# A hybrid diffusion step on one core: the modulation vectors summed over row blocks on ACT, POOL and DVE instead of in TensorE's accumulation

## The chip, the core and the metric

One core of one Trainium2 chip. Its engines are TensorE (PE, with its weight loads PEld), VectorE (DVE), ScalarE (ACT), GpSimd (POOL) and SyncE (SP, which here issues all transfers); SBUF and PSUM are the on-chip memories. The time of a run is the device time in microseconds; lower is better.

## The reference, cut to what matters

Two layers of a backbone run on 128 context tokens and 512 latent tokens of 1024 features. Each layer has three branches (a bidirectional S5, a windowed and a global attention), which gates merge, then an output projection, a norm, a squared-ReLU MLP of 4096 and a norm. Six modulation vectors of 1024 values each come from a conditioning vector, one for the context tokens and one for the latent tokens:

```
m = jax.nn.silu(cond) @ w_mod + b_mod          # cond: 1024 values; w_mod: 1024 x 6144; 2 conds
sh1, sc1, g1, sh2, sc2, g2 = split(m, 6)
h  = x * (1 + sc1) + sh1                       # before the input projection
x  = layer_norm(alpha * x + g1 * f)
h2 = x * (1 + sc2) + sh2                       # before the MLP
x  = layer_norm(alpha * x + g2 * (relu(h2 @ w_up) ** 2 @ w_down))
```

All is float32.

## The kernel before

The kernel is written layer by layer: `phase_a` holds everything up to the merged branches, `phase_b` the output projection, the MLP and the two norms. Weights come in packed tiles of 128x1024 (512 KB). `raw_tile` (line 112) loads one into a ring of four buffers, which all weights share in program order; `wtile` (line 126) splits it into a high part, written by ACT (line 123), and the exact rest, written by DVE (line 124), and every product with activations is three matmuls, high by high, high by low and low by high (lines 159 to 161 and 170 to 172). The modulation is not split: its matmuls (line 187) take float32 as it is.

`mods_steps` (line 175) makes the vectors. It is a generator: its caller takes one step at a time beside other work. A round is 2048 columns (two vectors); a step is one row block k of 128 rows, two raw tiles. `scond[:, k, :]` holds the conditioning vectors after SiLU, 128 rows by 32 columns, of which two are not zero. Four matmuls a step, each with 32 result partitions (a quarter q of the round's columns, at partitions 32q) and 512 columns, multiply it by the raw tile. In the second layer the eight steps accumulate in one PSUM bank and ACT copies the sums out (line 192). In the first layer (`acc=True`) each step has a bank of its own, and DVE adds it to the row so far (line 190). Then four transposes (line 197) and an add of the bias (line 198) put the vectors on the partitions, and the two gates also go to DRAM as rows (lines 203 to 211).

The first two vectors of the first layer are made elsewhere (`mods0`, line 516, untouched). `mods_steps` makes its other two rounds as the `side` of `branch` (line 1072), which takes a step after each of its 16 products: first for the window branch, which runs among the blocks of the global attention, then for the S5 branch. For the second layer it makes all three rounds during the first layer's MLP: `ahead` (line 1253) takes a step beside most weight tiles, in turn with the tables of the S5 branch (`s5_prep`, line 274) while these last. Those tables use DVE, POOL and PE.

[...] In the MLP `pg` hands out `g` and `sc` banks.

The order of each engine's instructions isn't the order of the code: `TileContext(..., schedule_with_timeline_sim=True)` has a planner lay out every engine's queue beforehand, by a simulated timeline in which earlier code goes first. On the chip each queue then runs in that fixed order.

Of the kernel before, what the change touches and what calls it, by code (L numbers as in the profile page):

```python
# [15 lines left out]
NT = 5                      # token tiles of 128: 0 the prompt, 1..4 the sample  # L16
D = 1024
NCH = 84                    # chunk columns: [pad, 16 prompt, pad, pad, 64 sample, pad]
# [5 lines left out]
AHEAD = ((0, 1, 4, 2, 4, 1), (1, 0, 1, 2, 4, 1))   # gates worked out ahead: beside the queries, the scan, beside its outputs, around the GLU, by layer  # L24
# [3 lines left out]
SPLITS = ((0, 3), (3, 5))   # token-tile ranges of a feature-major product  # L28


def net(tc, I, O, depth=DEPTH, dbg=None):
# [37 lines left out]
    # ---------------------------------------------------------------- constants  # L69
# [19 lines left out]
    V.memset(mh, -0.5)  # L89
    scond = base.tile([128, 8, 32], F32, name="scond")  # L90
# [17 lines left out]
    # persistent work  # L108
# [8 lines left out]
    def split(hi, lo, src, half=False):  # L117
        """src (or src / 2) as a high part and the exact rest"""
        if half:
            S.activation(hi, src, AF.Copy, scale=0.5)  # L120
            V.scalar_tensor_tensor(lo, src, 0.5, hi, op0=ALU.mult, op1=ALU.subtract)
        else:
            S.activation(hi, src, AF.Copy)  # L123
            V.tensor_tensor(lo, src, hi, op=ALU.subtract)  # L124

    def wtile(src, K, slot=None):
        """a packed weight tile [128, 1024] of K row blocks as its high and low parts: [(hi, lo)] by row block"""
# [17 lines left out]
    def tok(a, t0, t1):  # L145
        """the token tiles t0..t1 of a view [128, NT, 128], or of the views of the two parts of SPLITS"""
        if not isinstance(a, tuple):
            return a[:, t0:t1, :]
        i = 0 if t0 < SPLITS[0][1] else 1
        return a[i][:, t0 - SPLITS[i][0]:t1 - SPLITS[i][0], :]  # L150

    def mm_fm(out, ws, acts, t0, t1, ks=None, first=True, last=True):
        """feature-major: out [128 f, tokens] += w[k].T @ act[k]; ws[k] = (hi, lo) [128, 128];
        acts[k] = (hi, lo) views of the tokens"""
# [8 lines left out]
    def mm_tm(out, ws, acts, t, first=True, last=True):  # L163
        """token-major: out [128 tok, n] += act[k][:, t].T @ w[k]; ws[k] = (hi, lo) [128, n]"""
# [9 lines left out]
    # ---------------------------------------------------------------- adaLN modulation  # L174
    def mods_steps(l, rounds, tmp, tmp2=None, acc=False):
        """the modulation vectors of a layer, 2048 columns a round, one row block of the weight a step"""
        if rounds[0] == 0:
            SY.dma_start(bmodT, I["bmodT"][:, l])
        for r in rounds:
            p = None if acc else ppv()  # L180
            mrow = tmp()
            for k in range(8):
                if acc:
                    p = pg()
                ws = [raw_tile(I["w_mod"][l, r, k, h]) for h in range(2)]
                for q in range(4):
                    T.matmul(p[32 * q:32 * q + 32, :], scond[:, k, :], ws[q // 2][:, (q % 2) * 512:(q % 2) * 512 + 512],
                             start=(acc or k == 0), stop=(acc or k == 7))
                if acc and k > 0:
                    V.tensor_tensor(mrow, mrow, p, op=ALU.add)  # L190
                elif acc or k == 7:
                    S.activation(mrow, p, AF.Copy)  # L192
                if k < 7:
                    yield
            pc = pg() if acc else ppv()
# [6 lines left out]
            # the gates as rows  # L202
            for q in range(4):
                vec = 2 * r + q // 2
                if vec in (2, 5):
                    P = slice(32 * q, 32 * q + 2)
                    brow = (tmp2 or tmp)()
# [6 lines left out]
    def affine(l, w):  # L214
        """affA/affB[l][:, w]: h = xhat * A + B; w 0: before w_in, 1: before w_up"""
# [11 lines left out]
    # ---------------------------------------------------------------- h: transposed, modulated, split  # L227
    def new_h():
        """high and low parts, each in the two parts of SPLITS"""
        return tuple(tuple(wp.tile([128, 8, t1 - t0, 128], F32R, name=n + str(i), tag=n + str(i), bufs=1)  # L230
                           for i, (t0, t1) in enumerate(SPLITS)) for n in ("hh", "hl"))

# [23 lines left out]
    # ---------------------------------------------------------------- layer norm of a token tile  # L256
    def ln_stat(st):
        """mean, rstd, - mean rstd from the bn_stats of the chunks"""
# [8 lines left out]
    def ln_tile(z, st):  # L267
        """z [128, 1024] -> (z - mean) * rstd in place; st: bn_stats of its chunks"""
# [4 lines left out]
    # ---------------------------------------------------------------- S5 tables (weights only)  # L273
    def s5_prep(l, pp, after=None, use=None):
# [25 lines left out]
        def poly(o, r, cs):  # L300
            """cs: from the highest power, to the constant"""
# [8 lines left out]
        def expm1(o, x, plus1=False):  # L310
            """exp(x) - 1 (or exp(x)): x = k ln2 + r"""
# [8 lines left out]
            tt(q, q, r, ALU.add)                       # e^r - 1  # L320
# [3 lines left out]
            p2 = ti.bitcast(F32)                       # 2^k  # L324
# [12 lines left out]
        # sin and cos - 1 of th: th = q 2pi + r, a = r/4, two doublings  # L337
# [19 lines left out]
        # powers of lam_bar: Pw[:, ri, k, g], k = 0..8; n = lam_bar - 1  # L357
# [27 lines left out]
        # b_bar = (lam_bar - 1) / lam * b  # L385
# [13 lines left out]
        # ec[t]: fwd lam^(t+1), bwd lam^(8-t);  ei[j]: fwd lam^(7-j), bwd lam^j  # L399
# [12 lines left out]
        for b in range(8):  # L412
# [31 lines left out]
            # C lam^e and its negated imaginary part  # L444
# [10 lines left out]
            # lag kernel of these four groups; stationary columns: [full | fwd | bwd]  # L455
# [15 lines left out]
            # input operator, built with states on partitions and transposed  # L471
# [20 lines left out]
    # ---------------------------------------------------------------- phase A  # L492
    def phase_a(l, h):
# [9 lines left out]
        if l == 0:  # L503
# [3 lines left out]
            # the rows of a partial sum over four row blocks: one from each strip  # L507
# [4 lines left out]
            # the first three row blocks of the S5 input go along  # L512
# [3 lines left out]
            def mods0(g_):  # L516
                """shift and scale of 256 features"""
# [57 lines left out]
        # entry states by chunk column, the backward direction turned round inside each segment  # L575
# [12 lines left out]
        def s5_in(b, io):  # L588
            """what the chunks of four groups add to the states"""
# [15 lines left out]
        # ---- S5 input, to the chunked layout  # L605
# [27 lines left out]
        def s5_states():  # L633
            """the states at the chunks' starts"""
# [6 lines left out]
            # ---- scan over chunks: entry[i + 1] = lam^8 entry[i] + v, prompt and sample side by side, in pairs:  # L641
            # w = lam^8 v[i] + v[i + 1]; entry[i + 2] = lam^16 entry[i] + w one after the other; the entries between them
# [11 lines left out]
            def pairs(src, dst):  # L654
                """dst + 2 k += lam^8 (src + 2 k), all 41 pairs of columns"""
# [26 lines left out]
            # final states of the prompt  # L682
            fin = sp.tile([128, 2, 2, 32], F32, name="fin", tag="sa", bufs=1)[:, 0].rearrange("p a b -> p (a b)")
            S.activation(fin, st[:, 17].rearrange("p a b -> p (a b)"), AF.Copy)
            # the backward direction back into chunk order
# [11 lines left out]
        # ---- k, v, q of the window branch  # L697
# [3 lines left out]
        # the rotation with the weights of the query norm, and the sums of squares of the queries  # L701
# [8 lines left out]
        def rope_apply(out, src, n, t, e, tab=None):  # L710
            """out[., h, 64] = src * C + swap(src) * S; src [128, n, 64], sample tile t - 1"""
# [14 lines left out]
        def chunk(name, i):  # L726
            """two packed tiles: the 256 columns i of a token-major weight, K = 1024"""
            return wtile(I[name][l, 2 * i], 4) + wtile(I[name][l, 2 * i + 1], 4)

        def kv_gemm(i, side=iter(())):  # L730
# [15 lines left out]
            if i == 1:  # L746
                # the norm of the keys
# [6 lines left out]
            # the rotation of the sample's keys  # L754
# [9 lines left out]
        def q_gemm(i, dst, side=iter(()), cs=(0, 1)):  # L764
            for c in cs:
                ws = chunk("w_q", 2 * i + c)
                for t in range(NT):
# [10 lines left out]
                    else:  # L778
                        # the norm's factor of a row and head goes with the scores
# [14 lines left out]
        def gate(i, ft, out_fn, side=iter(())):  # L794
            """tanh(gate / 2): sigmoid(gate) = (1 + that) / 2; the halves go with the sums"""
# [8 lines left out]
        def gates_ahead(i, fts):  # L804
            """gates ahead of their use, kept in DRAM; half a gate a step"""
# [25 lines left out]
        # ---- window attention, beside the scan  # L831
        # ---- attention
# [4 lines left out]
        def keys(i):  # L837
            """K^T high and low, on both partition halves; V as [high | low]"""
# [3 lines left out]
            # cached keys and values  # L842
# [20 lines left out]
        def queries(qt):  # L863
            """qt [128, 512] token-major -> scaled, transposed, by head: high and low part on the two partition halves"""
# [11 lines left out]
        def attend(i, t, qs, KH, KL, VV, y):  # L876
            """token tile t of branch i; y slab [128, NT, 4, 128]"""
# [6 lines left out]
            # contiguous runs of key columns  # L884
            runs = []
            n1 = 4 if len(blks) < 5 else 3          # blocks in a bank of their own; the two heads share one for the rest
# [7 lines left out]
            stat = atp[0].tile([128, 4, 8], F32, name="stat", tag="stat", bufs=2)      # -max | sums | second sums | 1 / sum  # L894
            ng, sm, sx, rs = (stat[:, j] for j in range(4))
            for v in range(2):
                po = ppv()
                for pr in range(2):
# [3 lines left out]
                    # a bank for each of the two heads, and one for what does not fit  # L902
# [53 lines left out]
                # the products with the high and the low part of v sit on the two partition halves  # L956
# [14 lines left out]
            # 1 / sum of each row, spread over the features of its head  # L971
# [25 lines left out]
        # gates of the window branch fill the tensor engine beside the scan  # L997
# [10 lines left out]
        # ---- outputs of the chunks  # L1008
# [35 lines left out]
        # ---- second half: the merged branches  # L1044
# [12 lines left out]
        def y_views(ft):  # L1057
            """(natural tokens [c, t], same of yT) for the prompt and the sample"""
# [415 lines left out]
```

## Time and profile before

| | |
|---|---|
| median of 3 timed runs | 2419.13 us (2417.3 to 2419.89) |
| span of the profiled execution | 2422.9 us |
| mean granted TensorE clock | 0.977 |
| busy: PE, DVE, ACT, POOL | 95%, 62%, 41%, 23% |
| moved by DMA | 278.25 MB, 115 GB/s |

The profiled execution has no time of its own beside its span, from its first to its last instruction. In the rows, L187 is line 187 of the kernel. `out<-in` gives tiles by name, `128x512` partitions by elements. [...] A row's idle time is that of the engine just before these instructions, with what ended it. Stretches are counted from the span's start.

### The profile page before, as it was taken

The page shows a single profiled execution, that of the slowest core. Times are in us where ns is not written, and L with a number is a line of the kernel's source. Part 1 is how long each engine was busy: PE and PEld are TensorE (multiplying, and loading weights), DVE is VectorE, ACT ScalarE, POOL GpSimd, SP SyncE. Part 2 cuts the span into 40 slices and gives each one's busy share as a digit, 9 for nine tenths or more (in the row PEclk, how much of TensorE's full clock was granted, in tenths as well). Part 3 has the DMA queues.
Part 4 walks back from the last instruction along what each step waited for, and adds up shares of the span by engine and source line. Part 5 has one row for each costly group of instructions (what it writes and reads, how often), then busy time and mean ns, then how long its engine had stood idle before and what let it go on. Part 6 is the DMA issues. An engine that isn't in the chain of part 4 may idle for free.

```text
span 2422.9 us, 43760 instructions
## 1 busy us (share of the span) xinstructions
PE 2305.5 (95%) x17304; PEld 2201.2 (91%) x17304; DVE 1501.1 (62%) x3091; ACT 992.3 (41%) x2320; POOL 567.6 (23%) x665
## 2 busy tenths in 40 slices
PE   7887999999999999999999889999999889999997
PEld 4777897799999999999999889999999889999997
DVE  6887854766357966654664766466744873444467
ACT  2324655574344333222234256467643343232221
POOL 2555700001024211100541651000102350000056
PEclk8998999999999999999999999999999999999999
DMA  7423236612241344455326223511222332222221
GB/s 261 144 82 103 97 111 225 230 68 89 72 158 54 115 164 157 162 174 200 122 97 189 72 67 111 158 61 71 77 75 72 146 100 75 76 73 79 71 73 59
DMA packets 126381, 278.25 MB, mean 115 GB/s; under 512 B 40640, under 2 KB 60224, under 8 KB 126176
## 3 DMA queue, kind: packets, MB, share of 16 engines
q1 hardware_dynamic: 126176, 275.45, 33.5%
q8 instruction: 136, 2.23, 0.4%
q14 instruction: 69, 0.57, 0.1%
HBM read 240.97 MB, written 38.63 MB: 115 GB/s over the span
## 4 chain that ended last, share of the span: by engine, by line
PE 78%; DVE 8%; POOL 6%; DMA 3%; ACT 2%; issue 2%; SPq 0%; DVEq 0%; ACTq 0%; POOLq 0%
PE p_g L159 9%; PE p_g L161 9%; PE p_g L160 9%; PE p_sc L170 4%; PE p_sc L172 4%; PE p_sc L171 4%; PE p_g L170 4%; PE p_sc L160 4%; PE p_g L171 4%; PE p_sc L161 4%; PE p_sc L159 4%; PE p_g L172 4%; PE p_pt L947 2%; PE p_g L1025 2%; POOL sa L677 1%
## 5 line engine op out<-in xcount | busy, mean ns | idle before, releaser
L124 DVE TENSOR_TENSOR wlo<-raw,whi 128x512 fp32r<-128x512 f32 x472 | 364.5, 785 | 194.4 <-ACT whi L123 188.6
L123 ACT ACTIVATE whi<-raw 128x512 fp32r<-128x512 f32 x472 | 293.5, 630 | 416.8 <-PE p_sc L172 138.8
L159 PE MATMUL p_g<-hh,whi 128*128 128x384 f32 (+1 forms) x1200 | 379.4, 316 | 2.8 <-ACT mt L802 2.6
L161 PE MATMUL p_g<-hh,wlo 128*128 128x384 f32 (+1 forms) x1200 | 377.4, 315 | 2.5 <-DVE wlo L124 2.2
L160 PE MATMUL p_g<-hl,whi 128*128 128x384 f32 (+1 forms) x1200 | 377.8, 315 | 0.0
L159 PEld LDWEIGHTS p_g<-hh,whi 128*128 128x128 f32 x1200 | 227.8, 190 | 10.1 <-ACT rl L1274 5.8
L161 PEld LDWEIGHTS p_g<-hh,wlo 128*128 128x128 f32 x1200 | 227.7, 190 | 4.3 <-DVE wlo L124 3.7
L160 PEld LDWEIGHTS p_g<-hl,whi 128*128 128x128 f32 x1200 | 228.2, 190 | 0.6 <-issue 0.5
L159 PE MATMUL p_sc<-hh,whi 128*128 128x256 f32 (+1 forms) x672 | 209.1, 312 | 9.1 <-ACT hh L123 8.8
L160 PE MATMUL p_sc<-hl,whi 128*128 128x256 f32 (+1 forms) x672 | 208.2, 310 | 4.1 <-DVE hl L124 4.1
L161 PE MATMUL p_sc<-hh,wlo 128*128 128x256 f32 (+1 forms) x672 | 208.4, 310 | 1.5 <-DVE wlo L124 1.5
L1090 POOL TENSOR_TENSOR mt<-sg,mt 128x640 f32<-128x640 f32 x24 | 41.2, 1719 | 652.1 <-DVE stat L934 272.4
L170 PE MATMUL p_sc<-whi,ff 128*128 128x256 f32 x680 | 192.9, 284 | 0.0
L172 PE MATMUL p_sc<-whi,ff 128*128 128x256 f32 x680 | 192.3, 283 | 0.0
L171 PE MATMUL p_sc<-wlo,ff 128*128 128x256 f32 x680 | 191.1, 281 | 0.0
L170 PE MATMUL p_g<-whi,hh 128*128 128x256 f32 x544 | 161.8, 299 | 10.8 <-DVE rt L785 6.6
L171 PE MATMUL p_g<-wlo,hh 128*128 128x256 f32 x544 | 161.3, 297 | 8.9 <-DVE wlo L124 8.6
L172 PE MATMUL p_g<-whi,hl 128*128 128x256 f32 x544 | 159.8, 295 | 0.0
L124 DVE TENSOR_TENSOR pl<-p_pt,ph 128x512 fp32r<-128x512 f32 (+1 forms) x176 | 102.8, 589 | 69.0 <-ACT ph L123 60.8
L159 PEld LDWEIGHTS p_sc<-hh,whi 128*128 128x128 f32 x672 | 131.0, 195 | 15.3 <-ACT hh L123 9.7
L159 PE MATMUL p_g<-act,whi 128*128 128x384 f32 x448 | 140.3, 313 | 3.7 <-ACT mtmp L192 2.3
L170 PE MATMUL p_g<-whi,ff 128*128 128x256 f32 x500 | 142.0, 284 | 0.0
(410 smaller groups left out, 6371.8 us busy)
## 6 DMA issues: line engine op xcount, KB each, us to landing
raw<-in_w_mod_dram SPq DMA_DIRECT2D x96, 512.0 KB
raw<-in_w_up_dram SPq DMA_DIRECT2D x64, 512.0 KB
raw<-in_w_down_dram SPq DMA_DIRECT2D x64, 512.0 KB
raw<-in_w_gate_dram SPq DMA_DIRECT2D x48, 512.0 KB
raw<-in_w_br_dram SPq DMA_DIRECT2D x24, 512.0 KB
raw<-in_w_q_dram SPq DMA_DIRECT2D x16, 512.0 KB
ctab_d<-prow SPq DMA_DIRECT2D x16, 512.0 KB
tab<-ctab_d SPq DMA_DIRECT2D x16, 512.0 KB
```

The source lines that it names most:

```text
L123: S.activation(hi, src, AF.Copy)
L124: V.tensor_tensor(lo, src, hi, op=ALU.subtract)
L159: T.matmul(out, wh, tok(ah, t0, t1), start=(first and k == 0), stop=False)
L160: T.matmul(out, wh, tok(al, t0, t1), start=False, stop=False)
L161: T.matmul(out, wl, tok(ah, t0, t1), start=False, stop=(last and k == n - 1))
L170: T.matmul(out, ah, wh, start=(first and k == 0), stop=False)
L171: T.matmul(out, ah, wl, start=False, stop=False)
L172: T.matmul(out, al, wh, start=False, stop=(last and k == n - 1))
L677: G.tensor_tensor(a[:, 0:ns], at(cur), lb(M[:, 0]), op=ALU.mult)
L947: T.transpose(p[:, (2 * (z - z0) + z_) * 128:(2 * (z - z0) + z_ + 1) * 128], Ps[z_][:, z * 128:(z + 1) * 128], ident)
L1025: T.matmul(o, ct[:, r_, q], st[:, :, r_, g_], start=False, stop=(r_ == 1))
L1090: G.tensor_tensor(mtv[:, ft], sg, mtv[:, ft], op=ALU.add)
```

## The change

Each raw tile of the modulation's weights is now multiplied by the conditioning value of its row (one scalar a partition) and added, element by element, to a running sum of 128x1024; only the sum over the 128 partitions is left to PE, which multiplies it by a column of ones. For the context's vector (c = 0) ACT multiplies and POOL adds; for the latent's (c = 1) DVE does both in one instruction. A half h of a round (one vector) is worked off over all eight row blocks before the next. A step is one raw tile in the first layer (16 a round instead of 8) and two in the second (8 as before). All sums and transposes go through the one `pv` bank. The first layer's `acc` form is gone.

```diff
+    onec = base.tile([128, 2, 32], F32, name="onec")
+    V.memset(onec, 0.0)
+    for c in range(2):
+        V.memset(onec[:, c, c:c + 1], 1.0)
...
-    def mods_steps(l, rounds, tmp, tmp2=None, acc=False):
+    def mods_steps(l, rounds, tmp, tmp2, part, step=1):
...
-            p = None if acc else ppv()
             mrow = tmp()
-            for k in range(8):
-                if acc:
-                    p = pg()
-                ws = [raw_tile(I["w_mod"][l, r, k, h]) for h in range(2)]
-                for q in range(4):
-                    T.matmul(p[32 * q:32 * q + 32, :], scond[:, k, :], ws[q // 2][:, (q % 2) * 512:(q % 2) * 512 + 512],
-                             start=(acc or k == 0), stop=(acc or k == 7))
-                if acc and k > 0:
-                    V.tensor_tensor(mrow, mrow, p, op=ALU.add)
-                elif acc or k == 7:
-                    S.activation(mrow, p, AF.Copy)
-                if k < 7:
+            for h in range(2):
+                sums = [part() for _ in range(2)]
+                for k in range(8):
+                    raw = raw_tile(I["w_mod"][l, r, k, h])
+                    s0, s1 = (scond[:, k, c:c + 1] for c in range(2))
+                    if k == 0:
+                        S.activation(sums[0], raw, AF.Copy, scale=s0)
+                        V.tensor_scalar(sums[1], raw, s1, None, op0=ALU.mult)
+                    else:
+                        z = part("mpr")
+                        S.activation(z, raw, AF.Copy, scale=s0)
+                        G.tensor_tensor(sums[0], sums[0], z, op=ALU.add)
+                        V.scalar_tensor_tensor(sums[1], raw, s1, sums[1], op0=ALU.mult, op1=ALU.add)
+                    if k % step == step - 1 and k < 7:
+                        yield
+                p = ppv()
+                for q in (2 * h, 2 * h + 1):
+                    for c in range(2):
+                        T.matmul(p[32 * q:32 * q + 32, :], onec[:, c, :], sums[c][:, (q % 2) * 512:(q % 2) * 512 + 512], start=(c == 0), stop=(c == 1))
+                S.activation(mrow[64 * h:64 * h + 64, :], p[64 * h:64 * h + 64, :], AF.Copy)
+                if h == 0:
                     yield
-            pc = pg() if acc else ppv()
+            pc = ppv()
...
-                          lambda: t640("br")...[:, 0:512], acc=True) if l == 0 else iter(())
+                          lambda: t640("br")...[:, 0:512],
+                          lambda n="mac": bp.tile([128, D], F32, name=n, tag=n, bufs=2 if n == "mac" else 1)) if l == 0 else iter(())
...
-                              lambda: mp.tile([128, 4, 128], F32, name="hf", ...)), s5_prep(...)]
+                              lambda: mp.tile([128, 4, 128], F32, name="hf", ...),
+                              lambda n="mac": mp.tile([128, D], F32, name=n, tag=n, bufs=2), 2), s5_prep(...)]
...
-    nc = bacc.Bacc("TRN2", target_bir_lowering=False, num_devices=1)
+    nc = bacc.Bacc("TRN2", target_bir_lowering=False, num_devices=1, dynamic_dma_scratch_size=1024)
```

`onec` is zero but for ones at `[:, c, c]`. The sums have two buffers (`mac`), ACT's products one in the first layer and two in the second (`mpr`). The last line makes the scratch for dynamic transfers smaller. The rest of the diff takes comments out.

## Rows read from the trace of the kernel before

**Rows 1.** The page's first part: busy us, share of the span, instructions.

```profile
PE 2305.5 (95%) x17304; PEld 2201.2 (91%) x17304; DVE 1501.1 (62%) x3091; ACT 992.3 (41%) x2320; POOL 567.6 (23%) x665
```

**Rows 2.** The page's chain that ended last: shares by engine.

```profile
PE 78%; DVE 8%; POOL 6%; DMA 3%; ACT 2%; issue 2%; SPq 0%; DVEq 0%; ACTq 0%; POOLq 0%
```

**Rows 3.** Stretches: length, busy us by engine, clock, DMA share, GB/s.

```profile
395.00:480.00 85.00, 80.59 (x545) 58.49 (x544) 59.73 (x131) 52.46 (x123) 0.00 (x0) 1.00 0.71 253
480.00:540.00 60.00, 59.91 (x440) 59.49 (x439) 41.73 (x92) 39.48 (x102) 0.00 (x0) 1.00 0.22 77
540.00:700.00 160.00, 158.67 (x1102) 157.17 (x1102) 76.34 (x137) 65.56 (x144) 25.29 (x15) 1.00 0.23 78
835.00:1100.00 265.00, 265.00 (x2177) 246.19 (x2176) 165.88 (x337) 81.72 (x164) 32.54 (x31) 1.00 0.51 170
1100.00:1170.00 70.00, 70.00 (x528) 62.21 (x527) 27.20 (x48) 18.36 (x35) 0.00 (x0) 1.00 0.49 178
```

(The engines are PE, PEld, DVE, ACT, POOL in this order, with their instructions.)

**Rows 4.** Instructions in order of time, PE at 835 us: start, us.

```profile
835.28 0.28 PE L172 MATMUL p_sc<-whi,ff 128*128 128x256 f32 x1
835.49 1.07 PE L187 MATMUL p_pv<-raw,scond 128*32 128x512 f32 x8
...
836.49 0.38 PE L170 MATMUL p_sc<-whi,ff 128*128 128x256 f32 x1
```

**Rows 5.** Groups of instructions by line, PE: busy us, mean ns, idle before.

```profile
L187 PE MATMUL p_pv<-raw,scond 128*32 128x512 f32 x192 | 25.6, 605 | 0.0
...
L187 PE MATMUL p_g<-raw,scond 128*32 128x512 f32 x128 | 22.2, 605 | 0.5 <-DVE mt L1088 0.5
```

**Rows 6.** Instructions in order of time, PE at 395 to 407 us.

```profile
402.36 0.44 PE L159 MATMUL p_g<-act,whi 128*128 128x384 f32 x1 [2.33 <-ACT mtmp L192]
...
405.24 1.05 PE L187 MATMUL p_g<-raw,scond 128*32 128x512 f32 x4
406.23 0.38 PE L159 MATMUL p_g<-act,whi 128*128 128x256 f32 x1
```

**Rows 7.** Groups by line and shape, whole span, of ACT, DVE and POOL.

```profile
L271 ACT ACTIVATE x<-x,ve 128x1024 f32<-128x1024 f32 x10 | 12.4, 1242 | 40.0 <-DVE ve L270 40.0
...
L1203 ACT ACTIVATE x<-x 128x1024 f32<-128x1024 f32 x5 | 5.3, 1059 | 0.6 <-DMA x<-in_x_dram 0.4
...
L124 DVE TENSOR_TENSOR wlo<-raw,whi 128x512 fp32r<-128x512 f32 x472 | 364.5, 785 | 194.4 <-ACT whi L123 188.6 <-PE p_g L160 3.9 <-PE p_pv L955 0.7
...
L190 DVE TENSOR_TENSOR mtmp<-mtmp,p_g 128x512 f32<-128x512 f32 x14 | 9.6, 684 | 9.2 <-PE p_g L187 5.6 <-ACT mtmp L192 3.4
...
L1088 DVE SCALAR_TENSOR_TENSOR mt<-mt,p_g 128x384 f32<-128x384 f32 x16 | 8.8, 550 | 9.6 <-PE p_g L161 9.5
...
L1088 DVE SCALAR_TENSOR_TENSOR mt<-mt,p_g 128x256 f32<-128x256 f32 x16 | 6.7, 418 | 8.6 <-PE p_g L161 8.5
...
L1367 DVE SCALAR_TENSOR_TENSOR acc<-acc,ve,rr 128x512 f32<-128x512 f32 x6 | 6.2, 1039 | 0.1
...
L1090 POOL TENSOR_TENSOR mt<-sg,mt 128x640 f32<-128x640 f32 x24 | 41.2, 1719 | 652.1 <-DVE stat L934 272.4 <-DMA raw<-in_w_gate_dram 232.1 <-DVE sg L1088 141.9
...
L1316 POOL TENSOR_TENSOR acc<-acc,x 128x512 f32<-128x512 f32 x20 | 30.3, 1541 | 0.0
```

**Rows 8.** Stretches with other work on POOL or DVE; columns as in Rows 3.

```profile
800.00:835.00 35.00, 35.00 (x242) 35.00 (x241) 31.31 (x151) 15.35 (x34) 0.00 (x0) 0.95 0.34 122
1170.00:1210.00 40.00, 40.00 (x304) 40.00 (x303) 31.99 (x35) 10.27 (x21) 30.39 (x20) 1.00 0.28 98
```

**Rows 9.** Groups by line and shape, DVE, 1170 to 1210 us.

```profile
L124 DVE TENSOR_TENSOR wlo<-raw,whi 128x512 fp32r<-128x512 f32 x10 | 14.9, 1525 | 0.0
...
L1297 DVE TENSOR_TENSOR acc<-acc,p_sc 128x512 f32<-128x512 f32 x3 | 2.1, 684 | 3.7 <-PE p_sc L172 3.7
```

**Rows 10.** One instruction in order of time, DVE at 837 us, POOL idle.

```profile
837.12 0.69 DVE L124 TENSOR_TENSOR wlo<-raw,whi 128x512 fp32r<-128x512 f32 x1
```

**Rows 11.** Instructions on one tile (scond): duration min/median/max, first and last start.

```profile
L92 ACT ACTIVATE scond<-condT x1: 216/216/216, 4.2 to 4.2; 128x16 f32<-128x16 f32 x1
```

More of the change, by code (lines that the diff above doesn't have):

```diff
@@ L206, in mods_steps @@
                     P = slice(32 * q, 32 * q + 2)
-                    brow = (tmp2 or tmp)()
+                    brow = tmp2()
                     SY.dma_start(brow[P, :], ap(I["b_mod"], (l * 6 + vec) * 1024 + (q % 2) * 512, [[0, 2], [1, 512]]))
@@ L1109, in phase_a @@
         mods = mods_steps(0, (1, 2), lambda: bp.tile([128, 512], F32, name="mtmp", tag="mtmp", bufs=1),
-                          lambda: t640("br").rearrange("p t n -> p (t n)")[:, 0:512], acc=True) if l == 0 else iter(())
+                          lambda: t640("br").rearrange("p t n -> p (t n)")[:, 0:512],
+                          lambda n="mac": bp.tile([128, D], F32, name=n, tag=n, bufs=2 if n == "mac" else 1)) if l == 0 else iter(())
         n1 = sum(AHEAD[l][:4])
@@ L1249, in phase_b @@
             nxt = [mods_steps(l + 1, range(3), lambda: mp.tile([128, 512], F32, name="mtmp", tag="mtmp", bufs=1),
-                              lambda: mp.tile([128, 4, 128], F32, name="hf", tag="hf", bufs=2).rearrange("p a b -> p (a b)")), s5_prep(l + 1, mp, x[:, NT - 1, D - 1:D])]
+                              lambda: mp.tile([128, 4, 128], F32, name="hf", tag="hf", bufs=2).rearrange("p a b -> p (a b)"),
+                              lambda n="mac": mp.tile([128, D], F32, name=n, tag=n, bufs=2), 2), s5_prep(l + 1, mp, x[:, NT - 1, D - 1:D])]
         calls = [0]
```

## The prediction

> **What bounds the kernel now.** I read the page's busy shares first, then its chain, then the stretches in which the changed code runs, then single instructions. PE is busy 95% of the span, DVE 62%, ACT 41%, POOL 23% [rows 1], and PE is 78% of the chain that ended last [rows 2]. The share of a whole span proves little, so the reader is to look at the stretches: the first layer's vectors are made at 395 to 480 us, the second layer's at 835 to 1170 us. In the second place PE is busy for every microsecond of 335, at full granted clock, with DVE at 58% and POOL at 10%; in the first PE is busy 80.6 of 85 us, and in the 220 us behind it 218.6 [rows 3]. So in all of them a microsecond of PE work taken out is a microsecond of time, for as long as no other engine fills up.
>
> **What goes from PE.** There are 40 steps of four float32 matmuls, 16 in the first layer and 24 in the second. The trace holds two records for each matmul. Four matmuls lie on four 32-column groups and run side by side. In the second layer's stretch the last ordinary matmul starts at 835.28, the eight records at 835.49, the next ordinary one at 836.49 [rows 4]: 1.21 us, of which 0.12 is the spacing that any matmul there has (265 us by 2177 matmuls [rows 3]). So a step costs 1.09 us, 24 of them 26.2 us. The first layer's steps are busy 22.2 us [rows 5], more than 16 x 1.09, because some are cut in two halves of four records, and a half takes as long as a whole (405.24 to 406.23 [rows 6]). With them goes a wait of 2.33 us, where PE's next matmul waited for the first copy of the sums, which stood behind other work on ACT [rows 6]. Together 24.5 us, and both layers 50.7 us.
>
> **What PE gets instead.** Ten groups (five rounds, two halves each) of four matmuls against the column of ones. Each group uses two column groups only, and each column group gets two matmuls one behind the other, so four records. Two records on each of two column groups took 0.99 us [rows 6]; four take twice that less the shared ends, I take 1.9 us, 19 us for ten. Bounds: 1.09 us if everything packs as now (11 us), 3.7 us if the eight records run one by one at half of 0.99 us less the edges (37 us). The transposes behind them stay. PE's net relief is 50.7 - 19 = 31.7 us: 17 in the first layer, 15 in the second.
>
> **What ACT, DVE and POOL get.** 80 blocks of 128x1024 (32 and 48).
> - ACT: 80 products. A plain copy of that shape took 1.06 us, one with a scale and a bias per partition 1.24 [rows 7]; I take 1.15, 92 us in all, 55 in the second layer's 335 us, where ACT is busy 100: 155 of 320, hidden.
> - DVE: 80 products with sum. A 128x384 of this operation took 0.55 us and a 128x256 0.42 [rows 7], so 128x1024 comes to 1.21; 97 us, 58 in the second layer. Twice the 128x512 of the tail that met POOL is 2.08 [rows 7], the upper bound. The 14 adds into the old row go (9.6 us [rows 7]).
> - POOL: 70 adds. 128x640 took 1.72 us [rows 7], by columns 2.75 for 1024; 193 us, 115 in the second layer. Upper bound twice the crowded 128x512, 3.08 [rows 7].
> - POOL and DVE hold each other up. At 1170 to 1210 us POOL is 30.4 us busy; ten splits of 128x512 on DVE took 1.525 us there against 0.69 alone, 8.4 us lost, while DVE's adds that read PSUM stayed at 0.68 [rows 8 to 10]. So DVE loses about 0.28 us for each microsecond of POOL.
>
> [...]
>
> Second layer, sum for DVE: 193.1 now [rows 3] + 58 + 0.28 x 115 = 283 of 335 - 15 = 320 us, 89%. From 1100 us, where a step comes with every weight tile: 27.2 + 16 x 1.21 + 0.28 x 14 x 2.75 = 57 of 65 us (eight steps less, two sums more), 88%. Would PE suffer? At 800 to 835 us DVE is busy 31.3 of 35 us, at 1170 to 1210 DVE 32 and POOL 30.4 of 40, and PE has no idle time in either [rows 8]. So I count 3 us of stalls and keep 12 of 15.
>
> First layer: from 395 to 700 us DVE comes to 177.8 - 9.6 + 39 + 0.28 x 77 = 229 of 288 us, which is room. But two things bind here. The product's scratch tile has one buffer: ACT's next product waits for POOL's add, and behind it in ACT's queue stand the splits that PE needs. And the raw weight tiles are a ring of four that the modulation blocks share with all weights: a block is released by ACT and DVE, no longer by PE, so the ring turns no faster than POOL adds. The second round now runs beside the S5 branch product; there POOL has 14 x 2.75 plus eight merges of 1.72 us, 52 us (57 at the upper bound), for PE work of 48 us (192 branch and 144 gate matmuls at 0.144 us, 158.7 us by 1102 [rows 3]). I charge 10 us there and in the attention, and keep 7 of 17. Below nothing is excluded for this charge: no engine gets less to do than before but PE, and PE's relief is counted in full.
>
> At no cost: the new constant (three small memsets on DVE at the start; the first user of the tile set beside it waits on ACT until 4.2 us for a transfer [rows 11]; uncovered some 0.6 us), the two half copies of the sums on ACT, and the smaller scratch for dynamic transfers, since every transfer is issued by SP. No step moves past another on SP's queue but the first layer's second round, whose 16 blocks leave the stretch with the highest DMA share, 0.71 [rows 3].
>
> **Sum.** -31.7 + 3 + 10 = -18.7 us. The profiled execution shows its span, 2422.9 us, 3.8 above the median of the timed runs; the sum is a difference and is set against the median: 2419.1 - 18.7 = 2400 us.
>
> **Rivals.**
> 1. PE waits for the sums. The order of each engine's queue is fixed beforehand by a planner; where POOL's last add is later than planned, PE stands at the ones-matmul with its whole queue behind it. One late add each is 10 x 2.75 = 27.5 us: -31.7 + 27.5 = -4, about 2415, and with part of the other charges 2420. For it: in-order queues, POOL slower than planned when DVE crowds it. Against: the S5 tables already pass from POOL to PE in the second layer's stretch, and PE never waits there [rows 3].
> 2. All cover holds: no stalls, packed ones-matmuls. -50.7 + 11 = -40, 2379 us. Against it: PE already idles 4.4 us of the 85 [rows 3].
> 3. Slower: the pair DVE and POOL becomes the bound. If every add stopped DVE for its whole length, DVE would need 193.1 + 58 + 115 = 366 us in the second layer for 320 us of PE: +46 - 31.7 = +14, 2434 us. It begins to cost from a loss of 0.6 us for each microsecond of POOL (69 us of room by 115) and makes the kernel slower from 0.87. For it: the adds are twice as long as those at 1170 us and DVE has little idle time left. Against: 0.28 measured, and PE busy throughout beside it [rows 8].
>
> **How the numbers follow.** A measurement of this kernel tells 0.2%, 4.8 us, from no change. Forecast (2386 to 2412): 0.57. Rival 2 or near it (below 2386): 0.08. Rival 1 (2413 to 2424): 0.16, nearly all of it within 0.2%. Rival 3, also with stalls in the first layer (above 2424): 0.19. So faster 0.65, within 0.2% 0.15, slower 0.20. The range leaves out the outer tips of rivals 2 and 3: 2382 to 2432 us.
>
> **What would show it.** In the changed profile: the 320 records of step matmuls gone, 80 records of ones-matmuls instead, busy near 19 us; 70 POOL adds at 2.4 to 3.1 us; ACT products near 1.15 and DVE's near 1.3 to 2; the splits' mean on DVE above the 0.785 us of before by at most 0.1 [rows 7]; PE without idle time in the second layer's stretch. PE waits on POOL or on the sums of several microseconds speak for rival 1; DVE above 95% with PE waiting for splits, for rival 3. I am wrong if PE's busy time falls by less than 25 us, or if its idle time grows by more than 20.

## The result: 5.4% slower

The changed kernel takes 2549.2 us (median of 4, 2545.3 to 2553.7) against 2419.5: a ratio of 1.0536 (95% interval 1.0521 to 1.0551), 130 us slower where 19 us faster was forecast. The profiled execution's span is 2547.6 us.

The page's first part for the changed kernel, which answers to [rows 1]:

```profile
PE 2325.4 (91%) x17064; PEld 2227.5 (87%) x17064; DVE 1697.7 (67%) x3160; ACT 1074.6 (42%) x2405; POOL 764.9 (30%) x735
```

From the page's groups the splits and the new work of POOL and DVE (busy us, mean ns, idle before), and then, from PE's groups by line, the ones-matmuls:

```profile
L129 DVE TENSOR_TENSOR wlo<-raw,whi 128x512 fp32r<-128x512 f32 x472 | 391.4, 845 | 183.2 <-ACT whi L128 176.7
...
L198 POOL TENSOR_TENSOR mac<-mac,mpr 128x1024 f32<-128x1024 f32 x70 | 191.9, 2741 | 514.4 <-ACT mpr L197 307.7
...
L199 DVE SCALAR_TENSOR_TENSOR mac<-raw,scond,mac 128x1024 f32<-128x1024 f32 x70 | 135.6, 1937 | 36.7 <-DMA raw<-in_w_mod_dram 36.4
```

```profile
L205 PE MATMUL p_pv<-mac,onec 128*32 128x512 f32 x80 | 20.2, 598 | 1.8 <-DVE yg L977 1.8
```

The price list was right for POOL's add, 2.74 us, and for the ten groups of ones-matmuls, 20 us. What failed is the cover. PE's idle time, its span less its busy time, grew from 117 to 222 us [rows 1]. Its busy time rose too, from 2305.5 to 2325.4 us, though 48 us of step matmuls [rows 5] went and 20 came: the matmuls that both kernels have took some 47 us more (2305.5 - 48 against 2325.4 - 20). That goes with the clock: the mean granted clock fell from 0.977 to 0.959. So the 125 us between the two spans are 105 us of standing and 47 us of slower matmuls, less the 28 us of relief.

Setting the same instructions of both traces side by side, the changed kernel is 3 us ahead or level until the global attention, 83 us late at the first layer's output projection, 133 us late when its MLP ends, and between 124 and 133 us late from there on. So there are two losses, one in each place where vectors are made. Two stretches of the changed kernel (PE, PEld, DVE, ACT, POOL busy, granted clock, DMA share, GB/s) stand for them, the second layer's first; before, PE idled 5.8 us from 395 to 700 us and nothing from 835 to 1170, with a granted clock of 1.00 in both [rows 3]:

```profile
840.00:1304.00 464.00, 408.32 (x3048) 390.23 (x3047) 384.59 (x629) 180.32 (x315) 185.77 (x100) 0.94 0.42 142
406.00:537.00 131.00, 99.53 (x583) 83.98 (x581) 81.29 (x188) 86.39 (x232) 0.08 (x1) 0.90 0.02 7
```

In both PE stands, and a part of both, 55 of the 464 us and 27 of the 131, runs at the lower of the two granted clocks that the trace records, 0.50 and 1.00 (0.94 and 0.90 on the mean). In the first layer's stretch DMA's share is 0.02 and no engine is full: hardly a weight comes in for 131 us. SP's queue shows it first, then POOL's, then the instructions that end it, all in order of time (start us, us); the last row is from the view of SP's waits (us in total, times, longest):

```profile
403.61 8.25 SPq L119 DMA_DIRECT2D raw<-in_w_mod_dram  x2
424.27 0.33 SPq L997 DMA_DIRECT2D rt<-q_d  x1
540.31 0.33 SPq L119 DMA_DIRECT2D raw<-in_w_br_dram  x1
...
403.66 2.41 POOL L198 TENSOR_TENSOR mac<-mac,mpr 128x1024 f32<-128x1024 f32 x1 [1.26 <-ACT mpr L197]
540.42 3.02 POOL L198 TENSOR_TENSOR mac<-mac,mpr 128x1024 f32<-128x1024 f32 x1 [134.35 <-ACT mac L193]
...
536.63 0.43 DVE L977 TENSOR_TENSOR yg<-p_pv,yt 64x256 f32<-64x256 f32 x1
537.20 1.92 PE L205 MATMUL p_pv<-mac,onec 128*32 128x512 f32 x8 [1.84 <-DVE yg L977]
539.13 1.15 ACT L193 ACTIVATE mac<-raw,scond 128x1024 f32<-128x1024 f32 x1 [2.97 <-PE p_pv L205]
...
SPq L119 <- DVE mac L194: 119.2, 7, 115.3
```

The first half's eight blocks are summed at 406 us, but their ones-matmul starts at 537, when DVE has taken the attention's last result out of the `pv` bank (`p_pv`, one bank, which the attention's ten results fill one after the other; in the code the attention stands ahead of these steps). Until then the sums keep both `mac` buffers, so ACT and DVE cannot begin the next half, whose blocks stand in the ring of raw tiles. SP's next load waits 115 us until DVE lets go of one of them (L194 is DVE's first product of a half), and POOL waits 134 us. Meanwhile the attention runs nearly alone, without most of the gates and branch products that filled PE beside it before.

### The profile page after: what moved, and what is told of

Its sections match the earlier page's. It is cut to its first block, busy times and chain, and to the rows that moved or that the text cites. A ratio compares the mean times of both kernels' runs of the same rounds, so it can differ in the third digit from the quotient of the medians.

```text
span 2547.6 us, 43696 instructions
## 1 busy us (share of the span) xinstructions
PE 2325.4 (91%) x17064; PEld 2227.5 (87%) x17064; DVE 1697.7 (67%) x3160; ACT 1074.6 (42%) x2405; POOL 764.9 (30%) x735
## 5 line engine op out<-in xcount | busy, mean ns | idle before, releaser
L129 DVE TENSOR_TENSOR wlo<-raw,whi 128x512 fp32r<-128x512 f32 x472 | 391.4, 845 | 183.2 <-ACT whi L128 176.7
L164 PE MATMUL p_g<-hh,whi 128*128 128x384 f32 (+1 forms) x1264 | 400.8, 317 | 10.7 <-ACT sg L1146 4.6
L166 PE MATMUL p_g<-hh,wlo 128*128 128x384 f32 (+1 forms) x1264 | 398.6, 316 | 5.8 <-DVE wlo L129 5.2
L165 PE MATMUL p_g<-hl,whi 128*128 128x384 f32 (+1 forms) x1264 | 398.7, 316 | 1.3 <-DVE hl L129 1.3
L198 POOL TENSOR_TENSOR mac<-mac,mpr 128x1024 f32<-128x1024 f32 x70 | 191.9, 2741 | 514.4 <-ACT mpr L197 307.7
L175 PE MATMUL p_sc<-whi,ff 128*128 128x256 f32 x708 | 203.5, 287 | 2.3 <-ACT whi L128 2.3
L177 PE MATMUL p_sc<-whi,ff 128*128 128x256 f32 x708 | 203.1, 287 | 0.0
L164 PE MATMUL p_sc<-hh,whi 128*128 128x384 f32 (+1 forms) x608 | 191.1, 315 | 12.9 <-ACT hh L128 12.9
L165 PE MATMUL p_sc<-hl,whi 128*128 128x384 f32 (+1 forms) x608 | 189.7, 312 | 3.2 <-DVE hl L129 3.2
L166 PE MATMUL p_sc<-hh,wlo 128*128 128x384 f32 (+1 forms) x608 | 189.1, 311 | 0.0
L199 DVE SCALAR_TENSOR_TENSOR mac<-raw,scond,mac 128x1024 f32<-128x1024 f32 x70 | 135.6, 1937 | 36.7 <-DMA raw<-in_w_mod_dram 36.4
```

The lines of the kernel that those rows point to most:

```text
L164: T.matmul(out, wh, tok(ah, t0, t1), start=(first and k == 0), stop=False)
L165: T.matmul(out, wh, tok(al, t0, t1), start=False, stop=False)
L166: T.matmul(out, wl, tok(ah, t0, t1), start=False, stop=(last and k == n - 1))
L175: T.matmul(out, ah, wh, start=(first and k == 0), stop=False)
L177: T.matmul(out, al, wh, start=False, stop=(last and k == n - 1))
L198: G.tensor_tensor(sums[0], sums[0], z, op=ALU.add)
```

## The experiments

Each ran beside the kernel before on its chip; times are medians, ratios are to that kernel. The kernel before took 2416.0 to 2420.4 us there, so where two kernels are compared below, each is taken by its distance to its own kernel before. All but three change the second layer alone and make the first layer's vectors as before; the three say so.

**The bank.**

```diff
-                p = ppv()
+                p = ppv() if l else pg()
...
-            pc = ppv()
+            pc = ppv() if l else pg()
```

> The changed kernel, but in the first layer the ones-matmuls and the transposes use the two g banks, as before, not the one pv bank. Bank theory (the sums wait for the pv bank that the global attention holds, keep both sum buffers, and the raw blocks of the next half stand in the ring so that no weight is loaded from 405 to 540 us): the first ones-matmul comes before 430 us, the stretch without transfers goes, and the time falls by 60 to 85 us, to 2465 to 2490. Rival, POOL's adds at 2.75 us a block turn the ring too slowly whatever the bank: less than 20 us gained, 2530 to 2550.

Measured: 2482.4 us, 1.028 (1.026 to 1.031): 66 us slower than before instead of 130. Two banks in place of one were worth 63 us. The ones-matmuls of the first layer (first and last start), and the same 131 us as above:

```profile
L205 PE MATMUL p_g<-mac,onec x32: 592/592/617, 409.6 to 633.0; 128*32 128x512 f32 x32
```

```profile
406.00:537.00 131.00, 111.66 (x727) 105.06 (x726) 102.11 (x163) 90.64 (x199) 32.32 (x13) 0.91 0.32 108
```

They start at 410 us, not 537; transfers go on (0.32 for 0.02). The bank theory holds. PE still idles 19 of the 131 us.

**The second layer alone**: the first layer's vectors made as before.

> Only the second layer's vectors are made in the new way; the first layer's are made as before, on PE. If the two losses are separate: about 50 us slower than before, 2460 to 2480. If the second layer's loss was a consequence of the first's (other order of the queues): within 15 us of 2419.

Measured: 2457.1 us, 1.017 (1.015 to 1.019): 41 us, somewhat less than expected, and separate from the first layer's.

**Without POOL's adds.**

```diff
-                        G.tensor_tensor(sums[0], sums[0], z, op=ALU.add)
```

> As the second-layer kernel, but POOL's adds are left out (the context's sum is then its first block alone); ACT still makes all products, DVE all of its own. Lock theory (POOL's adds of 2.75 us hold up DVE's instructions): DVE's multiply-adds fall from 1.87 to about 1.3 us, the splits from 0.94 to below 0.8, and at least 35 of the 50 us go: at most 2435. Ring theory (ACT and DVE stand in front of modulation blocks that have not landed): ACT's waits for these blocks stay near 120 us and at most 15 us go: 2450 or more.

Measured: 2401.5 us, 0.994 (0.993 to 0.996): 56 us less than with the adds and 14 us faster than before, the 15 us of PE relief that the forecast has for this layer (the context's sum is not made here, so this shows the price and is no version to use). The stretch with the adds, and the groups in it of DVE's splits, multiply-adds and an add that reads PSUM:

```profile
840.00:1160.00 320.00, 288.96 (x2244) 276.86 (x2243) 275.56 (x437) 119.10 (x204) 126.79 (x63) 0.95 0.45 154
```

```profile
L129 DVE TENSOR_TENSOR wlo<-raw,whi 128x512 fp32r<-128x512 f32 x70 | 64.7, 939 | 1.5 <-ACT whi L128 1.4
L238 DVE SCALAR_TENSOR_TENSOR mac<-raw,scond,mac 128x1024 f32<-128x1024 f32 x32 | 58.6, 1833 | 15.1 <-DMA raw<-in_w_mod_dram 15.1
...
L1351 DVE TENSOR_TENSOR acc<-acc,p_sc 128x512 f32<-128x512 f32 x16 | 10.8, 677 | 0.0
```

The same without them:

```profile
840.00:1160.00 320.00, 317.48 (x2544) 304.33 (x2543) 249.64 (x468) 143.03 (x243) 42.98 (x31) 1.00 0.52 177
```

```profile
L129 DVE TENSOR_TENSOR wlo<-raw,whi 128x512 fp32r<-128x512 f32 x82 | 60.7, 752 | 3.4 <-ACT whi L128 3.4
L237 DVE SCALAR_TENSOR_TENSOR mac<-raw,scond,mac 128x1024 f32<-128x1024 f32 x39 | 50.0, 1282 | 32.7 <-DMA raw<-in_w_mod_dram 32.5
```

PE idles 31 us of 320 with the adds and 2.5 without; the multiply-add takes 1.83 against 1.28, the split 0.94 against 0.75, the add from PSUM stays at 0.68. ACT still stood 104 us in front of blocks that had not landed, and the loss was gone all the same. Over the whole of both traces, PE's idle time is 39 us longer with the adds (154.7 against 115.4), and the same 17160 matmuls are busy 15 us longer (their pages stand further below), at a granted clock of 0.95 in this stretch instead of 1.00. Together that is the 54 us by which the spans differ.

**Loads a step ahead.** A step loads the two raw tiles of the next one into a list `held`.

```diff
-                    raw = raw_tile(I["w_mod"][l, r, k, h])
+                    raw = held.pop(0)
...
+                    if k % step == step - 1:
+                        load()
```

> As the second-layer kernel, but each step loads the two raw blocks of the next step, so that they land before ACT and DVE ask for them; the work is the same. Ring theory: ACT's waits for these blocks fall from about 120 us to below 30 and at least 30 of the 50 us go: at most 2440. Lock theory: the waits go but the time stays within 15 us of the second-layer kernel, 2450 to 2480.

Measured: 2462.7 us, 1.019 (1.017 to 1.022), no gain. ACT's waits fell only from 121 to 100 us, so the edit didn't do what it was for; that these waits are not the price was shown by the kernel without adds.

**Contention or links?** Two kernels part them. In the first POOL adds the sum to itself, and the ones-matmuls take the latent's sum twice, so nobody reads what POOL makes:

```diff
-                        G.tensor_tensor(sums[0], sums[0], z, op=ALU.add)
+                        G.tensor_tensor(sums[0], sums[0], sums[0], op=ALU.add)
...
-                        T.matmul(..., onec[:, c, :], sums[c][...], ...)
+                        T.matmul(..., onec[:, c, :], sums[1][...], ...)
```

> As the second-layer kernel (2457 us), but POOL adds the running sum to itself and nothing reads it: the ones-matmuls take the latent's sum for both, and ACT's products are read by nobody. POOL's 42 adds have the same shape and place; only their links to ACT and PE are gone. Lock theory (DVE and POOL hold each other up at SBUF): the loss stays, 2440 to 2465, DVE's multiply-adds at 1.7 to 1.9 us. Link theory (ACT waits for POOL's buffers, PE for POOL's last add): the loss goes as without adds, 2400 to 2415.

In the second POOL writes zeros over ACT's product three times instead of adding it:

```diff
-                        G.tensor_tensor(sums[0], sums[0], z, op=ALU.add)
+                        for _ in range(3):
+                            G.memset(z, 0.0)
```

> As the second-layer kernel, but instead of each add POOL writes ACT's product over with zeros three times (about 3 us, the context's sum is then its first block alone): POOL is as long busy and ACT's next product waits for it as before, but POOL reads nothing from SBUF. Lock theory (POOL's reads hold up DVE's): 2400 to 2420, multiply-adds near 1.3 us. Link theory, or a lock that POOL's writes take too: 2440 to 2465.

Measured: 2453.1 us, 1.014 (1.012 to 1.017), and 2412.3 us, 0.998 (0.996 to 0.999). The stretch of each, the first with its splits and multiply-adds, and the page's first part of the second:

```profile
840.00:1160.00 320.00, 293.12 (x2303) 281.11 (x2302) 271.96 (x453) 124.81 (x213) 95.91 (x59) 0.96 0.47 158
...
L129 DVE TENSOR_TENSOR wlo<-raw,whi 128x512 fp32r<-128x512 f32 x71 | 70.8, 1011 | 2.2 <-ACT whi L128 2.1
L238 DVE SCALAR_TENSOR_TENSOR mac<-raw,scond,mac 128x1024 f32<-128x1024 f32 x33 | 42.3, 1281 | 32.3 <-DMA raw<-in_w_mod_dram 32.3
```

```profile
840.00:1160.00 320.00, 309.35 (x2451) 296.79 (x2451) 257.16 (x463) 139.72 (x239) 145.55 (x148) 0.99 0.51 175
...
PE 2285.4 (95%) x17160; PEld 2195.2 (91%) x17160; DVE 1574.8 (65%) x3142; ACT 1039.2 (43%) x2371; POOL 691.1 (29%) x791
```

Adds that nobody reads cost nearly all of it (36 of 41 us). POOL as long busy as with the adds, and still between ACT's products, but only writing, gives most of it back: this kernel is 4.5 us faster than before, where the one without POOL's work was 14 us faster. So it is the contention of POOL's reads with DVE; what the remaining 10 us are, POOL's writes or ACT's wait for them, these runs do not part. One part missed: in the first kernel the multiply-adds stayed at 1.28 us, and the splits took the loss (1.01 us).

**Both sums on DVE**, nothing on ACT and POOL; in the first layer with the g banks, in the second, each alone:

```diff
...
-                        z = part("mpr")
-                        S.activation(z, raw, AF.Copy, scale=s0)
-                        G.tensor_tensor(sums[0], sums[0], z, op=ALU.add)
-                        V.scalar_tensor_tensor(sums[1], raw, s1, sums[1], op0=ALU.mult, op1=ALU.add)
+                    for sm_, s_ in zip(sums, (s0, s1)):
...
+                            V.scalar_tensor_tensor(sm_, raw, s_, sm_, op0=ALU.mult, op1=ALU.add)
```

> New in the first layer alone, with the g banks, and both sums on DVE (two multiply-adds a block, no product on ACT, no add on POOL); the second layer as before. If POOL's adds were what the first layer still lost beside the bank: 17 us of PE relief shows in part, 2402 to 2412. If DVE's load itself holds PE up (about 246 of 288 us): 2418 to 2435.

> New in the second layer alone, both sums on DVE, no ACT product, no POOL add. DVE has some 315 us of work for 320. If DVE's time as such is the price, whoever causes it: PE waits for splits and the time is 2425 to 2450. If the price was only the mixing with POOL: 2402 to 2415.

Measured: first layer 2427.1 us, 1.004 (1.003 to 1.006); second layer 2409.8 us, 0.997 (0.995 to 0.998), 7 us faster than before and the one version here that beats it with the whole computation. First the stretch of 395 to 480 us of the former, then that of the second layer of the latter, with the page's first part:

```profile
395.00:480.00 85.00, 68.80 (x455) 61.49 (x454) 69.51 (x122) 46.06 (x104) 0.00 (x0) 0.96 0.45 154
```

```profile
840.00:1160.00 320.00, 316.86 (x2518) 301.65 (x2517) 296.25 (x531) 98.38 (x197) 43.42 (x31) 1.00 0.52 177
...
PE 2292.8 (95%) x17160; PEld 2199.2 (91%) x17160; DVE 1606.4 (67%) x3190; ACT 993.9 (41%) x2323; POOL 578.0 (24%) x665
```

In the second layer's stretch DVE is busy 93% of the time, more than with POOL's help (86%), and PE stands 3 us, not 31. Over the whole kernel DVE is busy even less than with POOL's help, 1606 us against 1629 (its page stands below): POOL took 42 multiply-adds off DVE and cost it more than that. In the first layer DVE is busy 82% of the stretch, the attention's exponentials end 57 us later than before (the last starts at 634.9 us, then at 578.0), and PE works 69 of 85 us. That DVE's load is what holds the attention up there is not shown by a run of its own.

**The first layer alone with the g banks**, sums as in the change:

> New in the first layer alone, with the g banks, ACT's products and POOL's adds as in the change; the second layer as before. If the losses of the layers add (66 us with the g banks in both, 41 in the second alone): some 25 us slower than before, 2435 to 2450. Against the same with both sums on DVE (2427 us) that is what POOL's adds cost here; if they cost nothing in this stretch, 2420 to 2430.

Measured: 2439.3 us, 1.008 (1.006 to 1.010). That is 19 us slower than before, where both sums on DVE were 10 us slower: POOL's adds cost some 9 us here too. With the second layer's 41 us that makes 60 of the 66 us that the change loses with the g banks.

**The S5 tables behind the modulation**, first with the sums as in the change, then with both on DVE:

```diff
-                it = nxt[calls[0] % len(nxt)]
+                it = nxt[0]
```

> As the second-layer kernel (2457 us), but the modulation's steps all come before the S5 tables' steps, not in turn with them; the work is the same. Late-table theory (PE's queue stands at the tables' transposes, whose inputs DVE makes late because POOL holds it up; 30 of the 40 us that PE idles at 840 to 1200 us): without the mixing these waits go, at most 2430. Load theory (POOL's adds take more from DVE than a step's period has; now a step comes with every tile, 3.2 + 2.5 + 0.62 x 5.5 = 9.1 us of DVE in 7.7): PE waits for the splits themselves, 2445 to 2480.

> As the kernel with both sums of the second layer on DVE (2410 us), with the modulation's steps all before the S5 tables' steps. A step is then 3.2 + 5.1 = 8.3 us of DVE in 7.6 us of PE for the first 24 tiles, the tables have the rest. If DVE's load in a stretch decides: PE waits there, 2415 to 2430. If DVE may run behind for that long: 2400 to 2412.

Measured: 2466.9 us, 1.019 (1.018 to 1.021), and 2429.3 us, 1.004 (1.003 to 1.006). PE's longest waits (us in total, times, longest), first of the second-layer kernel with the tables in turn (840 to 1200 us), then of the kernel with the tables behind (800 to 1260 us):

```profile
PE p_pt L532 <- DVE prow L343: 13.1, 3, 5.6
PE p_pt L518 <- DVE Bs L512: 6.6, 1, 6.6
```

```profile
PE p_sc L176 <- DVE wlo L129: 14.2, 7, 5.0
PE p_g L166 <- DVE wlo L129: 12.5, 4, 8.7
PE p_g L176 <- DVE wlo L129: 7.1, 4, 2.3
```

PE no longer stands at tables but at the splits (36 us of such waits), and the time is no better. On DVE alone the kernel loses 16 us against the mixed order, as expected if DVE's load in a step's period decides; the tables are not the cause. The former shows single meetings; DVE and POOL in order of time:

```profile
902.93 2.61 DVE L129 TENSOR_TENSOR ff<-rl,ff 128x256 fp32r<-128x256 f32 x1
...
915.14 0.42 DVE L1329 TENSOR_TENSOR rl<-rl 128x256 f32<-128x256 f32 x1
915.47 3.41 DVE L238 SCALAR_TENSOR_TENSOR mac<-raw,scond,mac 128x1024 f32<-128x1024 f32 x1
...
902.00 3.25 POOL L237 TENSOR_TENSOR mac<-mac,mpr 128x1024 f32<-128x1024 f32 x1
915.14 2.66 POOL L237 TENSOR_TENSOR mac<-mac,mpr 128x1024 f32<-128x1024 f32 x1 [9.89 <-ACT mac L232]
```

A split of 256 columns, which alone takes 0.41 us (the shortest in the trace of the kernel before), starts 0.9 us into POOL's add and ends at 905.54, 0.3 us after it. The multiply-add that starts at 915.47, 0.3 us into the next add, needs 3.41 us instead of 1.28.

**Shorter adds.**

```diff
-                        G.tensor_tensor(sums[0], sums[0], z, op=ALU.add)
+                        for j in range(2):
+                            hs_ = slice(512 * j, 512 * j + 512)
+                            G.tensor_tensor(sums[0][:, hs_], sums[0][:, hs_], z[:, hs_], op=ALU.add)
```

> As the second-layer kernel (2457 us, DVE busy 1629 us in all, 70 more than without adds), but each of POOL's adds is made as two of 128x512: the same columns and nearly the same time on POOL, in pieces as short as those at 1170 us from which the 0.28 came. Length theory (a DVE instruction waits for the rest of the POOL instruction that it meets, so long adds cost more a microsecond than short ones): DVE's excess falls from 70 to some 35 to 45 us and the time to 2425 to 2442. If the loss goes by POOL's busy time whatever its pieces: excess 60 to 75 us, 2447 to 2465.

Measured: 2451.6 us, 1.014 (1.011 to 1.017). DVE's busy time in all, for whole adds, no adds and half adds:

```profile
PE 2299.6 (94%) x17160; PEld 2207.7 (90%) x17160; DVE 1629.0 (66%) x3142; ACT 1039.2 (42%) x2371; POOL 693.0 (28%) x707
```

```profile
PE 2284.5 (95%) x17160; PEld 2194.0 (91%) x17160; DVE 1559.5 (65%) x3142; ACT 1039.4 (43%) x2371; POOL 581.4 (24%) x665
```

```profile
PE 2295.8 (94%) x17160; PEld 2205.4 (90%) x17160; DVE 1622.0 (66%) x3142; ACT 1039.0 (43%) x2371; POOL 714.8 (29%) x749
```

The same 3142 instructions of DVE take 69.5 us more with whole adds and 62.5 with halves (this last trace is of the fastest of four executions, 2443 us; the others took 2452). The length theory's 35 to 45 us did not come: by the columns that POOL adds, the loss is nearly the same. But POOL's time did not stay the same either. The whole adds make POOL 111.6 us busier, so DVE loses 0.62 us for each of these; the halves make it 133.4 us busier, 0.47 for each. Shorter pieces do cost DVE less by POOL's time, and POOL takes longer over them.

## Why the prediction was wrong

1. **PE's relief** was right as a price: 1.92 us for a group of ones-matmuls where 1.9 was taken, and 14 us gained in the second layer once nothing stood against it. So were the prices of ACT (1.15 us) and of POOL (2.74). DVE's multiply-add alone takes 1.28 us, 1.21 was taken. But both signs that the forecast set for being wrong came: PE's busy time rose by 20 us where it was to fall by 25 or more, and its idle time grew by 105 us, where more than 20 was the sign. The rise is a term that the sum does not have: in the two stretches in which PE stood the granted clock was 0.90 and 0.94, where it was 1.00 before, and the matmuls that both kernels have took some 47 us more.
2. **The first layer, "I charge 10 us there and in the attention, and keep 7 of 17".** This step failed, by some 90 us: 83 lost in place of 7 gained. The ring was named as the danger, but priced at the rate of POOL's adds. The bank was not looked at: the change sends sums to `pv`, which the attention fills ten times first, so that the sums keep their two buffers, the raw blocks keep the ring, and the weights stay away. With the g banks 63 us of the whole kernel's loss were gone. Of the other 19 us of this layer some 9 are POOL's adds. The last 10 stay with both sums on DVE; that they come from DVE's load beside an attention that needs DVE for every block is argued from one trace, not shown.
3. **"DVE loses about 0.28 us for each microsecond of POOL"** is the second step that failed; it measures 0.62. The stretch it was read from already had more, since only the ten splits were counted. More lines of the kernel before from the same view as [rows 9]:

```profile
L209 DVE TENSOR_TENSOR mtmp<-mtmp,hf 2x512 f32<-2x512 f32 x2 | 3.4, 1720 | 0.1
...
L1275 DVE TENSOR_TENSOR rl<-rl 128x256 f32<-128x256 f32 x2 | 1.9, 963 | 0.0
...
L124 DVE TENSOR_TENSOR ff<-rl,ff 128x256 fp32r<-128x256 f32 x2 | 1.4, 686 | 1.0 <-ACT ff L123 1.0
```

   With 0.67 us alone for the first (its shortest in that trace) and 0.42 for the other two they add 3.7 us to the 8.4, so 0.4 by the same 30.4 us of POOL. From 0.4 to 0.62 the adds' length may have a part: the pieces in that stretch are 128x512, and with pieces of that size the added work cost 0.47. Put into the forecast's own sum, 0.62 gives 193 + 58 + 0.62 x 115 = 322 us of DVE for 320 us of PE: rival 3, said to begin to cost from 0.6. It cost 56 us (41 and the relief of 15), more than 2.
4. **"Would PE suffer?"** PE untouched at 800 to 835 and 1170 to 1210 us was taken to show that PE bears a DVE 89% busy. Those are 35 and 40 us. In 320 us with the adds PE stood 31 us with DVE at 86%; on DVE alone it stood 3 us at 93%. What the busy share hides is shown in part: a held instruction counts as busy (2.61 us for 0.41). Of the 56 us, 39 are PE's idle time and 15 its slower matmuls at the lower clock. Why a DVE with idle time left keeps PE waiting stays open. One reading, not tested, is that the planner counts DVE's own work when it lays out the queues but not the holding up, so that everything behind comes later than planned.
5. **Rivals.** Rival 3 named the mechanism of the second layer: it took 56 us less without POOL's adds. Single meetings look as its strict form has them, DVE stopped for as long as the add runs (2.61 us where 0.41 would do, 3.41 where 1.28 would). POOL's writes cost DVE 15 us in all (1574.8 against 1559.5 us busy) where its adds, which also read, cost 69.5. At 840 to 1160 us 24 copies with one input (`Bs<-Bb`) take 22.8 us beside the writes and 8.6 with neither writes nor adds, while the splits, with two inputs, take 0.76 us each (0.75 without) and the multiply-adds 1.35 (1.28). Over the layer the strict form isn't reached: DVE lost 0.62 us for each microsecond of POOL's whole adds and 0.47 of the halves; no run shows 1. Rival 1, PE waiting for POOL's last add, didn't happen: the wait for sums that did occur was for a bank. No rival had that.

## What to carry to other kernels

Before an accumulation moves to another place in PSUM or to buffers of its own, ask who holds that bank and those buffers at that time, and what queue stands behind them: here a chain of one bank, two buffers and a shared ring cost 63 us, where the arithmetic was to save 17. An elementwise add on POOL beside a DVE that splits from SBUF is not free work on an idle engine; here DVE paid 0.62 us for each microsecond of it, and the same sums on DVE alone left DVE less busy and the kernel 48 us faster. A busy share of 60% tells of room only if the added work does not stretch what is there: here DVE's splits went from 0.785 to 0.845 us each. And an engine that is made to wait can lose twice: here PE stood 105 us longer, and its remaining matmuls took some 47 us more at a lower granted clock (0.959 on the mean, 0.977 before).

## What the hardware showed that was not expected

POOL's memset of 128x1024 takes 0.96 us. Such writes made POOL 110 us busier and slowed DVE by 15 us in all, 14 of them in 24 copies with one input; adds that made it 112 us busier cost 69.5 us. With halves of the adds the multiply-adds take 1.58 us on the mean (1.83 at 840 to 1160 us beside whole adds, 1.28 alone), but nine tenths of the loss stayed (62.5 of 69.5 us), and POOL was busy longer over the halves (133.4 us against 111.6).
